# Norms in finer steps in program order, and low parts of weights partly made by adding transfers

## The chip, the cores and the metric

The kernel runs on one NeuronCore of one Trainium2 chip. Its time is device microseconds of one execution. In this text PE is TensorE (PEld its weight loads), DVE is VectorE, ACT is ScalarE, POOL is GpSimd, and SP is SyncE, which issues nearly all loads from HBM.

## What is computed

A two-layer decoder trunk on 544 tokens: 512 of a prompt and 32 of a sample group (8 sequences of 4), model width 1024, feed-forward width 2816. One layer is, with `layer_norm` after each sum:

```python
x = layer_norm(ALPHA * x + 0.5 * swiglu(x, ffn1_up, ffn1_down), ln1)
proj = x @ w_in + b_in                       # queries, keys, values, GLU halves, two gates
attn = window_attention(q, k, v, ...)        # window 128, ALiBi, sinks
c = causal_depthwise(u_a * sigmoid(u_g), conv_dw_w, conv_dw_b)     # 31 taps
c = silu(layer_norm(c, conv_ln))
mix = sigmoid(g_attn) * (attn @ w_attn_out) + sigmoid(g_conv) * (c @ w_conv_out)
x = layer_norm(ALPHA * x + mix @ w_out, ln2)
x = layer_norm(ALPHA * x + 0.5 * swiglu(x, ffn2_up, ffn2_down), ln3)
```

All in float32. The norms run over the model width, which lies on partitions.

## The kernel before

**Arithmetic.** A float32 product is made of three matmuls in a faster 32-bit form (`F32R`): each operand is split into a high part (a cast on ACT) and a low part (operand minus high part, on DVE), and high×high, high×low and low×high are summed in PSUM. Weights come from HBM as float32 in "raw" tiles of 128x1024 (512 KB, 5 buffers), and become a pair of tiles `wh`, `wl`. Activations are kept as pairs too: `X[p]` is the pair for 256 of the 1024 rows of the activations, p from 0 to 3. Nearly all large tiles share one pool, "pair", of 37 buffers.

**Units.** `unit(w, xs, hf)` multiplies one weight piece (256 output columns) with one half `hf` of the tokens: 272 columns in each half. It runs `kk` k-steps (8 for width 1024, 6 for the last group of a feed-forward network) of 6 matmuls each, and it writes one of three double-bank PSUM buffers. At each k-step it first calls `due()`.

**Order.** The Tile scheduler orders the instructions of each engine by a simulation of its own, except where they are pinned to program order. Two devices steer it by hand. `put_off(steps)` puts a list of steps with delays on `self.later`; `due()` calls those whose time has come by `self.clock`, which each k-step advances by 0.7; `flush()` calls whatever is left. And weights are prepared ahead: `W()` loads and splits pieces `la` ahead of use with `prep()`; inside a network `V()`, `fill()`, `step()` do so piece by piece.

**A network and its tail.** A feed-forward network starts with `up_first()`: four pieces (a0, u0, a1, u1; gate and up columns) for both halves of the tokens. Then `middle()` runs fast products (three of seven blocks of a Strassen-like form, pinned) and down units. Its last group, `gl`, has four pieces p of six k-steps, each in two raw tiles of four and two k-rows. They run in `tail()`: units of half 0 with `un(p, 0)`, then units of half 1. Each unit's result is added to `Y[p]` on DVE (L705), and `ln_sum` (L449) sums the `Y[p]`. The tail of `mix()`, behind the output projection, is the same with units of eight k-steps (norm 2).

**A norm** (`ln_fin`) has three steps per half, each with a stop on PE:
- `centre`: fold of the sum (DVE, L461), a matmul with ones for the mean (L463), four subtractions on DVE (L468), four squares on ACT (L472), three adds on DVE (L474);
- `newton`: fold (L481), tiny matmuls with ones (L485), 14 tiny DVE operations of an inverse square root (`rsqrt`, L507 to L521);
- `scale`: matmuls that spread the root (L493), four multiplications on DVE (L497), and per p `emit`: two activations on ACT with gain and bias (L530, for the convolution Silu in L1432), a high part on ACT (L441) and a low part on DVE (L442).

The next network's first units need these pairs: half 0 at once, half 1 four units later. Behind the second network and norm 2, factors `T` for the fast products are made from the normed values (`right`, L549 to L555).

**The norm behind the convolution** (in `mix`). The 30 taps of the depthwise convolution run on DVE (L1081) beside attention and projections. When the last are done, both halves are summed, and their norm runs beside eight units of gate pieces (`gate("gc", p, h)`, sigmoid on ACT in L1358). The output projection of the convolution follows (`co`), and needs all of it as pairs.

Of the kernel before, what the change touches and what calls it, by code (L numbers as in the profile page):

```python
# [24 lines left out]
NT = SEQ + NS  # L25
# [29 lines left out]
A1, A2, A3 = 4, 4, 2  # L55
FOLD = 1
FD = (1.4, 0.7, 2.1)
D_LN = (2.1, 3.5, 2.1)
RS_SEED, RS_A, RS_B = 0x5F1FFFF9, 2.38924456, 0.703952253
SAT = (3, 4, 5, 6, 7, 8, 9, 10)  # L60
TF = 0
# [38 lines left out]
class Ker:  # L100
    def __init__(self, ctx, tc, a):
        self.tc, self.nc, self.a = tc, tc.nc, a
        pool = lambda n, b, **k: ctx.enter_context(tc.tile_pool(name=n, bufs=b, **k))
        self.cp = pool("cp", 1)
        self.fp = pool("fp", FPB)
        self.sp = pool("sp", 4)
        self.wp = pool("wp", WPB)
        self.pp = pool("pp", PPB)
        self.mp = pool("mp", 4)
        self.ps2 = pool("ps2", 3, space=bass.MemoryType.PSUM)  # L110
        self.ps1 = pool("ps1", 2, space=bass.MemoryType.PSUM)
# [46 lines left out]
    def plan(self):  # L158
# [8 lines left out]

        def fast(key, w, j):
# [21 lines left out]
        def ffn(l, f):  # L190
            up, dn = a[f + "_up"][l], a[f + "_down"][l]
            for key in self.ffn_order(l, f):
                if key[0] == "s":
                    fast((l, f) + key, up, key[1])
                elif key[0] == "dn":
                    g, p = key[1:]
                    std((l, f) + key, dn, p * 256, r0=256 * sum(GROUPF[:g]), kk=2 * GROUPF[g])
                else:
                    std((l, f) + key, up, (DFF if key[0] == "u" else 0) + key[1] * 256)
# [93 lines left out]
    def steps(self, key, kk, raw):  # L293
# [19 lines left out]
        if kk:  # L313
            for k, t in enumerate(raw):
                w = t.shape[1] / 4
                out.append((1.0 * w, 0, 2, lambda k=k, t=t: hi(f"d{k}", t)))
                out.append((0, 1.2 * w, 0, lambda k=k, t=t: lo(f"d{k}", t)))
            return out, lambda: self.ready.append((key, [box[f"d{k}"] for k in range(len(raw))], kk))
# [86 lines left out]
    def ahead(self, n):  # L405

        while self.loaded < min(self.pi + n, len(self.pieces)):
            self.prep(True)
# [10 lines left out]
    def unit(self, w, xs, hf, pin=lambda i: i):  # L419
# [31 lines left out]
    def ln_fin(self, acc, Y, hf, emit):  # L451
# [7 lines left out]
        def centre():  # L459
            s = acc[0][:, :, hs]  # L460
            nc.vector.tensor_tensor(s[:, 0], s[:, 0], s[:, 1], op=ALU.add)  # L461
# [7 lines left out]
            for p in range(4):  # L469
# [3 lines left out]
                if p:  # L473
                    nc.vector.tensor_tensor(a, a, q, op=ALU.add)  # L474

        box = {}

        def newton():
            a = acc[1][:, :, hs]
            if FOLD:  # L480
                nc.vector.tensor_tensor(a[:, 0], a[:, 0], a[:, 1], op=ALU.add)  # L481
# [18 lines left out]
        return [(D_LN[0], centre), (D_LN[1], newton), (D_LN[2], scale)]  # L500
# [23 lines left out]
    def ln_out(self, X, l, vg, vb, T=None, func=AF.Identity):  # L524
        vec = self.vec[l]

        def emit(p, y, hs):
            for m in range(2):
                c = 2 * p + m
                self.nc.scalar.activation(y[:, m, hs], y[:, m, hs], func,  # L530
                                          scale=vec[:, vg + c:vg + c + 1], bias=vec[:, vb + c:vb + c + 1])
            xh, xl = X[p]
            self.split(xh[:, :, hs], xl[:, :, hs], y[:, :, hs])
            if T is not None and hs.stop == NT:
                if T:
                    T[-1] = T[-1]()
                T.append(self.right(y))
                if p == 3:
                    T[-1] = T[-1]()
# [37 lines left out]
    def ffn(self, l, f, XYT, vg, vb, last):  # L577
# [11 lines left out]
        def gated(w, h, hf, sa):  # L589
# [3 lines left out]
            self.split(h[0][:, :, hs], h[1][:, :, hs], sa)  # L593
# [6 lines left out]
        def up_first():  # L600
            ws = [self.W(l, f, k, j, la=A1 - 2 * j - (k == "u")) for j in range(2) for k in ("a", "u")]
            hs = [new_h(0) for j in range(2)]
            for hf in range(2):
                for j in range(2):
                    sa = silu(ws[2 * j], hf)
# [6 lines left out]
                    gated(ws[2 * j + 1], hs[j], hf, sa)  # L612
# [121 lines left out]
        up_first()  # L734
# [7 lines left out]
        def pre(hf):  # L742
            if hf == 0:
                ws.extend(self.V(l, f, "dn", gl, p) for p in range(4))
            else:
                self.ahead(A3)
# [4 lines left out]
        return self.tail(un, 0, Y, X, l, vg, vb, pre, f == "ffn2")  # L751
# [25 lines left out]
    def flush(self):  # L777
        for c in self.later:
            for _, fn in c[1]:
                fn()  # L780
        self.later = []

    def put_off(self, steps):
        self.later.append([self.clock + steps[0][0], deque(steps)])

    def tail(self, un, first, Y, XN, l, vg, vb, pre=None, fast=False):

        T = [] if fast else None
        emit = self.ln_out(XN, l, vg, vb, T)
        acc = self.pair(), self.pair()  # L790
        if pre:
            pre(0)
        for p in range(4):
            un(p, 0)
            if p < first:
                un(p, 1)
                self.ln_sum(acc, Y, 1, p)
            self.ln_sum(acc, Y, 0, p)
        self.put_off(self.ln_fin(acc, Y, 0, emit))
        if pre:  # L800
            pre(1)
        for p in range(first, 4):
# [3 lines left out]
        self.put_off(self.ln_fin(acc, Y, 1, emit))  # L806
        return XN, Y, T

    def final(self, un, Y, l, g, b, pre):
# [52 lines left out]
        for hf in range(2):  # L862
            pre(hf)
# [126 lines left out]
    def mix(self, l, XYT):  # L990
# [336 lines left out]
        k_unit(0)  # L1327
        g0[0]()
        g0[2]()
        values(range(2))  # L1330
# [98 lines left out]
        def c_out(p, y, hs):  # L1429
            for m in range(2):  # L1430
                c = 2 * p + m
                nc.scalar.activation(y[:, m, hs], y[:, m, hs], AF.Silu, scale=vec[:, V_CG + c:V_CG + c + 1],  # L1432
                                     bias=vec[:, V_CBETA + c:V_CBETA + c + 1])

        acc = self.pair(), self.pair()
        for hf in range(2):
            for p in range(4):
                self.ln_sum(acc, cl, hf, p)
            self.put_off(self.ln_fin(acc, cl, hf, c_out))
            for p in range(2 * hf, 2 * hf + 2):  # L1440
                for h2 in range(2):
                    gate("gc", p, h2, 36)
        self.flush()
        Y = []
        CH = []
        for p in range(4):
            h, lo = self.hl()
            CH.append((h, lo))
            for hf in range(2):
                self.split(h[:, :, sl(hf)], lo[:, :, sl(hf)], cl[p][:, :, sl(hf)])  # L1450
# [20 lines left out]
        return self.tail(un, TF, Y, XN, l, V_LN2G, V_LN2B, fast=True)  # L1471
# [38 lines left out]
```

## Time and profile before

| | us |
|---|---|
| median of 3 runs | 2594.34 (2584.23 to 2597.09) |
| profiled execution | 2583.82 |
| its span, first to last instruction | 2581.9 |
| PE busy | 2509.8 |
| DVE busy | 1877.7 |
| ACT busy | 1195.0 |
| POOL busy | 238.2 |

The mean granted clock of PE is 0.985 of its full rate; it was lower in short stretches only. PE is busy nearly everywhere, so the places to read are the short stretches in which it isn't. In the order of time those are, for layer 0: the start, the tail of the first network (380 to 420 us), one stretch in attention (near 600), the norm behind the convolution (780 to 820), norm 2 (900 to 940), the tail of the second network (1280 to 1300); layer 1 repeats them 1280 us later, and the kernel ends with `final()`, whose transposes and stores take the place of the last norm.

### The profile page before, as it was taken

The numbers are of one execution on the slowest core, as the hardware profiler recorded it, in microseconds if no ns is written. First come the engines' busy times: TensorE is split into PE (matmuls) and PEld (weight loads), VectorE is DVE, ScalarE is ACT, GpSimd is POOL, SyncE is SP. The second block draws the span as 40 slices with busy tenths as digits, with TensorE's granted clock in tenths as the row PEclk, the third lists the DMA queues.
The fourth block names the chain that finished last, engine by engine and source line by source line (L and its number), as shares of the span: only waits on it lengthen the run. The fifth ranks groups of instructions, "written<-read, shape, count | busy, mean of one in ns | idle before, by whom it ended". The sixth has DMA issues, their size and how long they took to land.

```text
span 2581.9 us, 47139 instructions
## 1 busy us (share of the span) xinstructions
PE 2509.8 (97%) x19846; PEld 2459.2 (95%) x19846; DVE 1877.7 (73%) x2955; ACT 1195.0 (46%) x2116; POOL 238.2 (9%) x323
## 2 busy tenths in 40 slices
PE   8999998999999999999899999999999999999997
PEld 8999998988999999999899999999899999999997
DVE  6766665997976577666667666669979666776665
ACT  4444434577426254434354434346873353444441
POOL 2000000722300000000100000016141000000000
PEclk9999999999999999999999999999999999999998
DMA  5333332231332223332503332322224222233321
GB/s 193 98 99 99 99 109 59 69 95 54 90 95 67 82 75 98 99 99 86 183 17 107 94 94 87 114 66 75 70 62 111 66 82 88 78 97 99 99 86 56
DMA packets 327140, 232.13 MB, mean 90 GB/s; under 512 B 43748, under 2 KB 324532, under 8 KB 326832
## 3 DMA queue, kind: packets, MB, share of 16 engines
q1 hardware_dynamic: 323088, 220.36, 28.6%
q0 software_dynamic: 3840, 8.76, 1.0%
q8 instruction: 155, 2.54, 0.4%
q14 instruction: 57, 0.47, 0.1%
HBM read 225.69 MB, written 9.16 MB: 91 GB/s over the span
## 4 chain that ended last, share of the span: by engine, by line
PE 84%; DVE 8%; ACT 3%; POOL 3%; issue 1%; DMA 1%; DVEq 0%; POOLq 0%; ACTq 0%
PE pa L652 17%; PE pa L432 17%; PE pa L434 17%; PE pa L433 17%; PE pb L652 13%; DVE pr L1081 3%; POOL f L1096 2%; DVE wl L278 1%; PE pa L1192 1%; PE pb L1221 1%; PE pb L1233 1%; DVE pr L442 1%; DVE pr L497 1%; ACT pr L1432 0%; ACT at L1206 0%
## 5 line engine op out<-in xcount | busy, mean ns | idle before, releaser
L432 PE MATMUL pa<-pr,wh 128*128 128x272 f32 x2624 | 766.0, 294 | 22.5 <-ACT pr L441 18.7
L434 PE MATMUL pa<-pr,wl 128*128 128x272 f32 x2624 | 764.2, 292 | 4.4 <-DVE wl L278 4.4
L433 PE MATMUL pa<-pr,wh 128*128 128x272 f32 x2624 | 761.3, 291 | 5.8 <-DVE pr L442 5.8
L432 PEld LDWEIGHTS pa<-pr,wh 128*128 128x128 f32 x2624 | 497.8, 190 | 30.1 <-ACT pr L441 21.8
L433 PEld LDWEIGHTS pa<-pr,wh 128*128 128x128 f32 x2624 | 501.4, 191 | 10.6 <-DVE pr L442 8.2
L434 PEld LDWEIGHTS pa<-pr,wl 128*128 128x128 f32 x2624 | 497.8, 190 | 5.3 <-DVE wl L278 5.0
L434 PE MATMUL pa<-pr,wd 128*128 128x272 f32 (+2 forms) x1408 | 406.9, 289 | 0.0
L432 PE MATMUL pa<-pr,wd 128*128 128x272 f32 (+2 forms) x1408 | 404.9, 288 | 0.0
L433 PE MATMUL pa<-pr,wd 128*128 128x272 f32 (+2 forms) x1408 | 404.6, 288 | 0.0
L1081 DVE SCALAR_TENSOR_TENSOR pr<-u,cw,pr 128x512 f32<-128x512 f32 x480 | 345.4, 769 | 2.0 <-ACT pr L1074 1.7
L433 PEld LDWEIGHTS pa<-pr,wd 128*128 128x128 f32 x1408 | 266.1, 189 | 0.0
L434 PEld LDWEIGHTS pa<-pr,wd 128*128 128x128 f32 x1408 | 264.5, 188 | 0.1
L432 PEld LDWEIGHTS pa<-pr,wd 128*128 128x128 f32 x1408 | 264.4, 188 | 0.2
L652 PE MATMUL pa<-pr,wa 128*128 128x272 f32 x1728 | 241.4, 289 | 0.0
L652 PE MATMUL pb<-pr,ws 128*128 128x272 f32 x1728 | 239.4, 288 | 0.0
L278 DVE TENSOR_TENSOR wl<-raw,wh 128x1024 fp32r<-128x1024 f32 x168 | 205.0, 1239 | 33.2 <-ACT wh L277 32.5
L652 PEld LDWEIGHTS pa<-pr,wa 128*128 128x128 f32 x1728 | 227.1, 188 | 0.0
L652 PEld LDWEIGHTS pb<-pr,ws 128*128 128x128 f32 x1728 | 224.9, 188 | 0.0
L277 ACT CAST wh<-raw 128x1024 fp32r<-128x1024 f32 x168 | 171.2, 1048 | 88.5 <-PE pa L433 36.1
L705 DVE SCALAR_TENSOR_TENSOR pr<-pa,pr 128x544 f32<-128x544 f32 (+2 forms) x160 | 115.3, 723 | 132.0 <-PE pa L434 130.4
L670 ACT COPY pb<-pa 128x272 f32<-128x272 f32 x72 | 26.6, 370 | 294.9 <-PE pa L652 294.9
L442 DVE TENSOR_TENSOR pr<-f,pr 128x544 fp32r<-128x544 f32 x124 | 89.1, 723 | 82.1 <-ACT pr L441 82.0
(226 smaller groups left out, 3741.8 us busy)
## 6 DMA issues: line engine op xcount, KB each, us to landing
raw<-in_ffn_up_dram SPq DMA_DIRECT2D x174, 512.0 KB, 4.0
raw<-in_ffn_down_dram SPq DMA_DIRECT2D x80, 512.0 KB, 3.4
raw<-in_w_in_dram SPq DMA_DIRECT2D x72, 512.0 KB, 3.9
raw<-in_w_in_dram SPq DMA_DIRECT2D x64, 128.0 KB, 2.9
raw<-in_w_attn_out_dram SPq DMA_DIRECT2D x32, 256.0 KB, 4.0
raw<-in_w_conv_out_dram SPq DMA_DIRECT2D x16, 512.0 KB, 3.5
raw<-in_w_out_dram SPq DMA_DIRECT2D x16, 512.0 KB, 4.4
raw<-in_ffn_down_dram SPq DMA_DIRECT2D x16, 256.0 KB, 2.7
```

The lines of the kernel that those rows point to most:

```text
L277: ins = self.nc.scalar.copy(wh, t)
L278: self.nc.vector.tensor_tensor(wl, t, wh.bitcast(F32), op=ALU.subtract)
L432: pin(self.nc.tensor.matmul(o, lhsT=wh, rhs=h, start=k == 0, stop=False))
L433: pin(self.nc.tensor.matmul(o, lhsT=wh, rhs=lo, start=False, stop=False))
L434: pin(self.nc.tensor.matmul(o, lhsT=wl, rhs=h, start=False, stop=k == kk - 1))
L442: pin(self.nc.vector.tensor_tensor(lo, src, hi.bitcast(F32), op=ALU.subtract))
L497: nc.vector.tensor_tensor(y[:, :, hs], y[:, :, hs], rb, op=ALU.mult)
L652: mm = lambda a, b, first=False, last=False: pin(nc.tensor.matmul(o, lhsT=a, rhs=b, start=first, stop=last, skip_group_check=True))
L670: pin(act.copy(A, b1))
L705: pin(nc.vector.scalar_tensor_tensor(Y[p][:, :, hs], ps, 0.5, Y[p][:, :, hs], op0=ALU.mult, op1=ALU.add))
L1081: self.last["cw"] = nc.vector.scalar_tensor_tensor(cc[:, m, 0:SEQ], u[:, m, k:k + SEQ], cw[:, 8 * k + c:8 * k + c + 1], cc[:, m, 0:SEQ], o ...
L1096: nc.gpsimd.tensor_tensor(pr[:, 4 * b:4 * b + 4, :], win, wv.unsqueeze(1).to_broadcast([128, DS, KC]), op=ALU.mult)
```

## The change

- **Program order.** A context `ordered()` makes each PE, DVE and ACT instruction inside it depend on the one traced before it on its engine, so the scheduler can't move it. It covers every tail, `up_first()` of every network but the first, the first units behind norm 1 in `mix` (keys, first GLU piece, first values), and the eight gate units with the convolution's norm.
- **Finer steps.** Tails start each half's norm after that half's units, with delays `D_T` instead of `D_LN`; both halves of the convolution's norm start together with delays `D_C` (the second's first delay is 14.0). The low parts of the normed values are no longer made in `emit`, but as four steps of their own (`D_LO`), and the factors `T` as five more (`D_R`). Folds move one step earlier: into `ln_sum` at p = 3, and to the end of `centre`. The convolution's pairs `CH` are made in its `emit` and not behind the flush. `flush()` now takes the remaining steps in order of time. A k-step advances the clock by 0.75.
- **Next weights.** `early()` loads the next piece and gives a step for each of its two tiles. In the tails of networks, one piece is split ahead of the units, with its low parts on DVE. Three more (six tiles, in every tail) are made at clock values `when` in the second half's units, at their end, and in the next network's first units, each in this way: ACT casts the high part, ACT writes minus the tile in the fast form to `wl`, and a transfer issued by POOL adds the raw tile to it in place.
- **Twin pieces.** Of the last down group, the two-row tiles of pieces p and p+1 are loaded into one raw tile by two transfers, so that two pieces have three tiles and not four.

```diff
+    @contextmanager
+    def ordered(self):
+        traced = self.nc.cur_bb.bb.instructions
+        start = len(traced)
+        last = {}
+        for i in traced:
+            last[i.engine] = i
+        self.hard = True
+        yield
+        self.hard = False
+        for i in traced[start:]:
+            if i.engine in (mybir.EngineType.PE, mybir.EngineType.DVE, mybir.EngineType.Activation):
+                self.tc.add_manual_dep(
+                    i, last[i.engine].name,
+                    mybir.DependencyInfo(mybir.DependencyClass.NoSync, mybir.DependencyReason.DATA), reason="ordered")
+            last[i.engine] = i
...
+D_T = ((2.6, 5.6, 4.0), (3.4, 5.6, 4.0))
+D_C = ((0.8, 5.6, 4.0), (14.0, 5.6, 4.0))
+D_LO = (1.7, 1.4, 1.4, 1.4)
+D_R = 2.0
...
+    def early(self, by_dma=True):
+        key, kk, raw = self.fetch()
+        ms = []
+        def one(t, end):
+            wh, wl = (self.pp.tile(list(t.shape), F32R, tag="pair", name=self.nm(n)) for n in ("wh", "wl"))
+            self.nc.scalar.copy(wh, t)
+            if by_dma:
+                self.nc.scalar.mul(wl, t, -1.0)
+                self.nc.gpsimd.dma_start(wl.bitcast(F32), t, accum_op=ALU.add)
+            else:
+                self.nc.vector.tensor_tensor(wl, t, wh.bitcast(F32), op=ALU.subtract)
+            ms.append((wh, wl))
...
-            self.clock += 0.7
+            self.clock += 0.75
...
+        if p == 3:
+            self.nc.vector.tensor_tensor(a[:, 0], a[:, 0], a[:, 1], op=ALU.add)
...
-            xh, xl = X[p]
-            self.split(xh[:, :, hs], xl[:, :, hs], y[:, :, hs])
...
+            h, lo = (x[:, :, hs] for x in X[p])
+            self.nc.scalar.copy(h, y[:, :, hs])
+            lows.append(lambda: self.nc.vector.tensor_tensor(lo, y[:, :, hs], h.bitcast(F32), op=ALU.subtract))
...
+    def tail_steps(self, un, Y, XN, l, vg, vb, when, first, T):
+        acc = self.pair(), self.pair()
+        def fin(hf):
+            lows = []
+            steps = self.ln_fin(acc, Y, hf, self.ln_out(XN, l, vg, vb, lows), D_T[hf])
+            steps += [(d, lambda i=i: lows[i]()) for i, d in enumerate(D_LO)]
+            if hf and T is not None:
...
+                steps += [(D_R, lambda i=i: factors(i)) for i in range(5)]
+            self.put_off(steps)
+        if first:
+            for fn in self.early(False):
                 fn()
         for p in range(4):
             un(p, 0)
             self.ln_sum(acc, Y, 0, p)
+        fin(0)
+        more = []
+        def tile():
+            if not more:
+                more.extend(self.early())
+            more.pop(0)()
+        for w in when:
+            self.put_off([(w, tile)])
+        for p in range(4):
             un(p, 1)
             self.ln_sum(acc, Y, 1, p)
         self.flush()
+        fin(1)
+        if more:
+            self.put_off([(1.0, tile)])
+        self.put_off([(4.5, tile), (0.1, tile)])
         return XN, Y, T
...
-        return self.tail(un, 0, Y, X, l, vg, vb, pre, f == "ffn2")
+        return self.tail(un, Y, X, l, vg, vb, (7.0, 9.5, 18.2), True, f == "ffn2")
...
+        with self.ordered():
+            for hf in range(2):
+                lows = []
+                steps = self.ln_fin(acc, cl, hf, c_out(lows), D_C[hf])
+                self.put_off(steps + [(d, lambda i=i, lows=lows: lows[i]()) for i, d in enumerate(D_LO)])
+            for p in range(4):
                 for h2 in range(2):
                     gate("gc", p, h2, 36)
-        self.flush()
+            self.flush()
...
-        return self.tail(un, TF, Y, XN, l, V_LN2G, V_LN2B, fast=True)
+        return self.tail(un, Y, XN, l, V_LN2G, V_LN2B, (7.0, 18.3, 24.2), False, fast=True)
```

## Rows read from the trace of the kernel before

**Rows 1.** The page, part 1: busy us (share of the span) xinstructions

```profile
PE 2509.8 (97%) x19846; PEld 2459.2 (95%) x19846; DVE 1877.7 (73%) x2955; ACT 1195.0 (46%) x2116; POOL 238.2 (9%) x323
```

**Rows 2.** Waits of PE: line, releaser, us in total, times, longest us

```profile
PE pa L432 <- ACT pr L441: 18.7, 7, 2.9
PE pb L493 <- DVE nw L521: 11.0, 3, 3.8
PE pb L485 <- DVE pr L481: 3.7, 3, 1.9
```

**Rows 3.** Windows of 20 us: busy us (instructions), granted clock, DMA share, GB/s

```profile
core 0: us, PE busy (x) PEld busy (x) DVE busy (x) ACT busy (x) POOL busy (x), PEclk, DMA share, GB/s
380.00:400.00 20.00, 14.27 (x112) 13.50 (x110) 15.65 (x36) 5.33 (x9) 0.15 (x1) 0.93 0.33 92
400.00:420.00 20.00, 17.71 (x122) 17.39 (x123) 13.24 (x29) 13.94 (x24) 0.00 (x0) 0.81 0.09 20
420.00:440.00 20.00, 19.86 (x162) 19.69 (x161) 10.48 (x16) 9.52 (x18) 0.00 (x0) 1.00 0.51 139
480.00:500.00 20.00, 19.91 (x174) 18.07 (x173) 19.90 (x45) 14.88 (x39) 18.96 (x25) 1.00 0.14 31
780.00:800.00 20.00, 19.11 (x155) 18.91 (x154) 13.10 (x29) 19.31 (x29) 0.00 (x0) 1.00 0.16 53
800.00:820.00 20.00, 17.15 (x127) 16.93 (x127) 14.29 (x18) 11.01 (x18) 0.00 (x0) 0.91 0.33 106
900.00:920.00 20.00, 19.43 (x149) 18.63 (x148) 16.65 (x22) 12.12 (x18) 0.00 (x0) 1.00 0.51 155
920.00:940.00 20.00, 16.94 (x136) 16.51 (x135) 12.63 (x31) 10.57 (x17) 0.00 (x0) 1.00 0.01 5
1280.00:1300.00 20.00, 10.77 (x54) 9.40 (x53) 16.32 (x37) 8.51 (x16) 0.00 (x0) 0.66 0.24 74
```

**Rows 4.** Timeline of DVE near 393: start, us, line, operation, out<-in, count

```profile
393.01 0.72 DVE L449 TENSOR_TENSOR pr<-pr,pr 128x544 f32<-128x544 f32 x1
...
397.28 2.62 DVE L497 TENSOR_TENSOR pr<-pr,pb 128x544 f32<-128x544 f32 x4 [1.06 <-PE pb L493]
```

**Rows 5.** Timeline of PE at 396, the spreading of the root

```profile
396.37 0.87 PE L493 MATMUL pb<-ident,nw 91*128 91x91 f32 x6 [3.75 <-DVE nw L521]
```

**Rows 6.** Timeline of DVE at 890: first and last of 14 Newton operations

```profile
890.06 0.16 DVE L507 TENSOR_SCALAR nw<-pb 91x3 f32<-91x3 f32 x1 [0.68 <-PE pb L485]
...
892.40 0.16 DVE L521 TENSOR_TENSOR nw<-nw,nw 91x3 f32<-91x3 f32 x1
```

**Rows 7.** Timeline of ACT, 760 to 810: squares, sigmoid, table load, Silu, copy

```profile
761.01 1.22 ACT L472 ACTIVATE f<-pr 128x544 f32<-128x544 f32 x2
...
771.00 0.87 ACT L1358 ACTIVATE pr<-pa,vec 128x272 f32<-128x272 f32 x2 [3.76 <-PE pa L434]
771.89 1.28 ACT L1432 ACT_TABLE_LOAD   x1
...
807.27 2.13 ACT L1432 ACTIVATE pr<-pr,vec 128x272 f32<-128x272 f32 x4
809.30 0.63 ACT L441 CAST pr<-pr 128x544 fp32r<-128x544 f32 x1
```

**Rows 8.** The page, part 5: low and high part of a weight tile

```profile
L278 DVE TENSOR_TENSOR wl<-raw,wh 128x1024 fp32r<-128x1024 f32 x168 | 205.0, 1239 | 33.2 <-ACT wh L277 32.5
L277 ACT CAST wh<-raw 128x1024 fp32r<-128x1024 f32 x168 | 171.2, 1048 | 88.5 <-PE pa L433 36.1
```

**Rows 9.** DMA issues of POOL's queue: count, KB each, median us to landing

```profile
out_new_conv_sample_dram<-in_state_conv_dram POOLq DMA_DIRECT2D x2, 832.0 KB, 12.5
at<-in_ln_g_dram POOLq DMA_DIRECT2D x1, 512.0 KB, 3.9
```

**Rows 10.** Timeline of POOL at 486: eight issues

```profile
485.74 4.20 POOL L1133 DMA_DIRECT2D out_new_v_sample_dram<-f  x8
```

**Rows 11.** Timeline of DVE ahead of the convolution's norm, 739 to 753

```profile
739.93 0.72 DVE L1424 TENSOR_TENSOR pr<-pa,f 128x544 f32<-128x544 f32 x1 [0.70 <-PE pa L434]
...
748.67 1.53 DVE L1081 SCALAR_TENSOR_TENSOR pr<-u,cw,pr 128x512 f32<-128x512 f32 x2
...
751.51 0.79 DVE L461 TENSOR_TENSOR pr<-pr 128x272 f32<-128x272 f32 x2
```

More of the change, by code (lines that the diff above doesn't have):

```diff
@@ L1 @@
 from collections import deque
[L2 removed]
+from contextlib import ExitStack, contextmanager
 import numpy as np
@@ L317, in steps, with whole @@
                 out.append((0, 1.2 * w, 0, lambda k=k, t=t: lo(f"d{k}", t)))
-            return out, lambda: self.ready.append((key, [box[f"d{k}"] for k in range(len(raw))], kk))
+            def whole():
+                ms = [box[f"d{k}"] for k in range(len(raw))]
+                if key[2] == "dn" and key[3] == len(GROUPF) - 1:
+                    if kk == 4:
+                        ms.append([x[:, 2:] for x in self.twin])
+                    else:
+                        self.twin = ms[1]
+                self.ready.append((key, ms, 6 if key[2] == "dn" and key[3] == len(GROUPF) - 1 else kk))
+            return out, whole
         La, Lu = raw
@@ L403, in after @@
                 mybir.DependencyInfo(mybir.DependencyClass.NoSync, mybir.DependencyReason.DATA), reason=key)
-    def ahead(self, n):
-        while self.loaded < min(self.pi + n, len(self.pieces)):
-            self.prep(True)
+    def early(self, by_dma=True):
[7 more added lines that the diff above has]
+                self.nc.gpsimd.dma_start(wl.bitcast(F32), t, accum_op=ALU.add)
+            else:
+                self.nc.vector.tensor_tensor(wl, t, wh.bitcast(F32), op=ALU.subtract)
+            ms.append((wh, wl))
+            if end:
+                self.ready.append((key, ms, kk))
+        return [lambda t=t, end=i == len(raw) - 1: one(t, end) for i, t in enumerate(raw)]
     def W(self, *key, la=LA):
@@ L592, in gated @@
             nc.vector.tensor_tensor(sa, ps, sa, op=ALU.mult)
-            self.split(h[0][:, :, hs], h[1][:, :, hs], sa)
+            if self.hard and not hf:
+                hh, hl = (x[:, :, hs] for x in h)
+                nc.scalar.copy(hh, sa)
+                self.put_off([(0.8, lambda: nc.vector.tensor_tensor(hl, sa, hh.bitcast(F32), op=ALU.subtract))])
+            else:
+                self.split(h[0][:, :, hs], h[1][:, :, hs], sa)
         def new_h(g):
@@ L733, in ffn @@
         turn = self.mark(l, f)
-        up_first()
+        if Y0:
+            with self.ordered():
+                up_first()
+                self.flush()
+        else:
+            up_first()
         Y += self.scaled(Y0)
@@ L740, in ffn, with pre @@
         ws = []
[L742 to L746, printed above, removed]
+        def pre():
+            ws.extend(self.V(l, f, "dn", gl, p) for p in range(4))
         un = lambda p, hf: down_unit(ws[p], gl, p, hf)
@@ L1326, in mix @@
         g0, g1, g2, g3 = (glu(p) for p in range(4))
[L1327 to L1330, printed above, removed]
+        with self.ordered():
+            k_unit(0)
+            g0[0]()
+            g0[2]()
+            values(range(2))
+            self.flush()
         k_unit(1)
@@ L1427, in mix, with c_out, emit @@
         cl = [C[p] for p in range(4)]
[L1429 to L1433, printed above, removed]
+        CH = [self.hl() for _ in range(4)]
+        def c_out(lows):
+            def emit(p, y, hs):
+                for m in range(2):
+                    c = 2 * p + m
+                    nc.scalar.activation(y[:, m, hs], y[:, m, hs], AF.Silu, scale=vec[:, V_CG + c:V_CG + c + 1],
+                                         bias=vec[:, V_CBETA + c:V_CBETA + c + 1])
+                h, lo = (x[:, :, hs] for x in CH[p])
+                nc.scalar.copy(h, y[:, :, hs])
+                lows.append(lambda: nc.vector.tensor_tensor(lo, y[:, :, hs], h.bitcast(F32), op=ALU.subtract))
+            return emit
         acc = self.pair(), self.pair()
```

102 lines of the change are left out of this document (55 added, 47 removed).

## The prediction

> **What bounds the kernel now.** The page's first part comes first: TensorE (PE) is busy 97% of the span, 2509.8 of 2581.9 us [rows 1]. So a change can win only where PE stands still or runs at its lower clock level. The waits of PE name such places [rows 2]: the first matmul of a unit waits for an activation's high part made by ScalarE (ACT), 18.7 us; a norm's last matmul waits for the Newton steps on VectorE (DVE), 11.0 us; the sum of squares comes late, 3.7 us. All belong to norms. Sizes come from the windows of 20 us [rows 3]. A full window holds 162 matmuls, so one costs 0.1235 us; a unit of eight k-steps (48 matmuls) costs 5.93, one of six 4.45, a step 0.74. Missing matmuls times 0.1235 is the loss, the clock included (granted 0.66 in the window at 1280, between the levels 1.2 and 2.4 GHz):
> - behind a first feed-forward network, 380 to 420: 90 missing, 11.1 us (twice, once a layer);
> - behind the second network of layer 0, 1280 to 1300: 108 missing, 13.3 us;
> - norm 2, 900 to 940: 39 missing, 4.8 us (twice);
> - norm of the convolution, 780 to 820: 42 missing, 5.2 us (twice).
> That is 55.5 us, the most there is to win.
>
> **Prices.** On half the columns a DVE add takes 0.72 (0.65 back to back, as in 2.62 for four) [rows 4]. The norm's own three stops cost PE about half a microsecond each (0.87 for six of the last stop, of two halves) [rows 5]. The 14 Newton operations take 2.5 us from first to last [rows 6]. On ACT a square costs 0.6, a 272-column activation 0.53, the copy of a high part about 0.54 where the next pass overlaps it: 1.6 for a pair [rows 7]. A weight tile costs 1.05 on ACT (high part) and, up to now, 1.24 on DVE (low part) [rows 8].
>
> **The tails behind the networks.** Before, the scheduler placed the first half's Newton and scale behind all units, so both halves' norms stood bare: DVE's L497 comes at 397, after PE's 3.75 us wait [rows 4, 5]. In the change PE must take them between k-steps at stated clock values. I put zero at the end of the first half's units, six k-steps each. Output add, sum, fold: 0.15 (hand-over, an estimate)+0.72+0.72+0.44, ready at 2.1; PE asks at 2.96. Four subtractions, squares behind each, three adds, fold: ready at 8.7; PE asks at 9.4. Newton runs 11.0 to 13.5 behind the second unit's two adds; PE asks at 14.4. Nothing waits. Multiplications 16.0 to 18.6, ACT's four pairs 16.7 to 23.1. The next network's first unit starts at 19.25 and needs pair 2's low part at 22.35; its subtraction stands in program order behind the last unit's output add and sums and ends at 22.95: **0.6 us of wait**. Second half: the early weight tile moved to the end of the units and its neighbour hold ACT from 23.1 to 27.2 (2.05 each: a cast and a multiplication by -1); the squares queue behind them, the sum is ready at 30.9 and PE asks at 30.05: **0.9 us**. Later steps have slack. I put 1.6 for a tail: two gain 11.1-1.6, together 19.0; the one at 1280 gains 11.7. Norm 2 has units of eight steps, 5.9 us more before the next network, and the same sums leave no wait; I allow 0.3, so 4.8-0.3 twice, 9.0. Moving DVE folds one step earlier costs nothing by itself: the 0.44 is in the sums above; without cover it would be 0.44 at a stop.
>
> **Low parts by transfers.** Six tiles in each of five tails leave DVE (1.24 each) and cost ACT about 1.05 more, a GpSimd (POOL) issue, and an adding transfer SBUF to SBUF, 512 KB. The trace has no such transfer. Below: 3.9 us, the plain load of the same size on that queue; above: 12.5, the longest that queue takes to land [rows 9]. It reads its destination too, so I take 6, near the row with the same queue and bytes. The third piece's tiles leave ACT at 25.1 and 27.2 and are needed at 33.6 and 36.6; the fourth's at 31.7 and 33.8, needed at 40.0 and 41.5. The least slack is 7.7: **no cost at 6**; at 12.5 about 4 us a tail. Below nothing: taking 1.24 off DVE could gain only where DVE ends a wait, which the sums already have. On POOL nothing but the convolution's clear and small state products is queued near them; SP's weight loads keep their order, but a raw buffer is held until its transfer lands, and the last of those loads has over 5 us in hand. The POOL queue issued eight transfers in 4.20 us, 0.52 each, while DVE was busy 19.90 of 20 us [rows 3, 10].
>
> The Trainium skill, "SBUF — State Buffer", section "SBUF: two separate sides" (its trap "DVE blocks DMA"), speaks against this: a DMA issued by GpSimd can starve for descriptors while DVE holds the shared port, 620 ns becoming 3,100. By it each issue is 2.5 us later, by estimate 8.5 to land and up to 0.8 us of wait a tail, 4 us in all. The row shows no such delay.
>
> **Twin pieces** (the last group's two short tiles loaded as one): 6 tiles instead of 8 a network, the same bytes and elements, four pair buffers fewer. I cost it at nothing: the window at 380 has 4.35 us of DVE and 14.7 of ACT idle to cover it [rows 3]; without that cover it is one cast, 1.05. The new clock step of 0.75 matches the 0.74 measured. The first two units' low parts put off by 0.8 are needed two units later: nothing.
>
> **The norm behind the convolution.** Here strict order cuts the other way. The last convolution taps keep DVE until 750.2 and the sums until 752.3 [rows 11], while the first gate unit starts near 745.8 (739.9 plus a unit). In the change the low parts of the second gate piece (2.4) move behind those sums, in program order ahead of the norm: sums end near 749.9, 4.1 after the unit's start; low parts 6.5; subtractions 9.1; adds and fold 11.7. PE asks for the mean after two k-steps and for the sum of squares at 7.9, and **waits 3.9 us** over the two. Second half, from the start of the third gate unit: sigmoid 0.9, two casts until 3.0, their low parts on DVE until 4.4, only then the first half's multiplications; the table load (1.28) hides, ACT's eight Silu and four copies run 5.1 to 11.5 [rows 7]. The second half's squares stand behind them: 11.5 to 13.9, fold 15.1. PE asks at 9.1 and **waits 6.0 us**. Behind PE are two gate units' sigmoids and nothing else that is late. Waits of such length cost clock: 0.91 of the window at 800 is 1.8 us lost [rows 3]; I add 2. So 12 replaces 5.2: a loss of 6.8, twice, 13.6. Its bounds: 0 (the taps end earlier and the sums with them, and ACT is free) and 17 (clock as at 1280, 6.8 lost). I take 12, since the taps run 4.4 us past the start of the gates [rows 11].
>
> **Sum.** 19.0+11.7+9.0-13.6 = 26.1. The profiled execution took 2583.8 (span 2581.9 and 1.9 around it), so 2557.7, say **2558**. The profiled time equals the lowest of the three runs, 10.5 below their median; a median of the changed kernel may lie as much above my number.
>
> **Rivals.**
> (A) The convolution's norm becomes free too. For: it now has eight gate units, 47 us, for two chains of 16. Against: the order of Silu and squares. No wait left: 2583.8-39.7-10.4 = 2534.
> (B) In-order waits eat half of the tails' gain: an ACT cast waiting for a raw tile holds the squares behind it. For: ACT carries 2.05 per early tile; against: five raw buffers and the slack above. 2583.8-19.9+13.6 = 2577.
> (C) Slower: the adding transfers run one behind another. Four tiles follow from 25.1, the last is needed at 41.5; the gain of 26 over five tails, 5.2 each, is gone when they land 5.4 us apart. At 6.5 apart a tail waits 9.6 us: 2583.8-26.1+48 = 2606. Against: the 3.9 us row includes latency that overlaps.
> (D) The order changes nothing that PE feels, because the scheduler's order already had it: 2584. Against: L497 at 397.
>
> **Chances.** Forecast 0.46 (2548 to 2568), A 0.28, B 0.12, D 0.06, C 0.08. Half a per cent, 13 us, is what a measurement here can tell from no change. Faster: 0.44+0.28+0.03 = 0.75; same 0.17; slower 0.08. Range 2530 to 2588: A with a few microseconds below, and B and D above; C is left out.
>
> **What would show it.** Windows as above: 380 to 420 and 1280 to 1300 with at most some 13 matmuls missing, clock 1.00; L497 of the first half well before the units end. In the convolution's norm PE should wait for DVE's L481 by about 4 and 6 us, Silu ahead of the squares on ACT. If that wait is absent, A; if PE waits for a DMA or low parts of weights, C; if for ACT casts, B. The prediction is wrong if PE waits at places without a norm, because buffers or loads moved.

## The result and the profile after

The changed kernel takes 2565.7 us beside 2594.8 before (medians of four executions each): a ratio of 0.989, 95% interval 0.985 to 0.993. One of its executions ran at a granted clock of 0.68 and took 3336.9 us; it counts in that median and not in the ratio, and the other three lie between 2561.5 and 2567.3, their median at 2564.1. The profiled execution took 2564.1 us (span 2562.3), 19.7 below that of before; the forecast was 26.1 below, at 2558.

The profile of the changed kernel: from its first part (busy us, share of the span, instructions), its DMA queues (packets, MB, share of 16 engines) and its DMA issues (count, KB each, median us to landing).

```profile
PE 2501.2 (98%) x19846; PEld 2454.7 (96%) x19846; DVE 1853.9 (72%) x2917; ACT 1229.7 (48%) x2138; POOL 266.5 (10%) x353
...
q0 software_dynamic: 8160, 24.49, 4.3%
...
L459 POOL DMA_DIRECT2D wl<-raw x30 | 26.4, 881 | 1303.4 <-DVE pr L534 947.4
...
wl<-raw POOLq DMA_DIRECT2D x30, 512.0 KB, 5.7
```

PE's busy time fell 8.6 us against [rows 1] and the span 19.6, so 11 us of what was won is time in which PE stood still and the rest is time in which it ran slowly. The adding transfers, which no row of before showed, are 30 and land in 5.7 us.

PE's waits in the changed kernel (line and releaser, us in total, times, longest). In its numbering L508 is the fold ahead of the mean, L534 the fold ahead of the sum of squares, L579 the last Newton operation, L592 the low part of a normed value, and L313 the low part of a weight tile:

```profile
PE pb L543 <- DVE pr L534: 17.2, 7, 6.5
PE pa L491 <- DVE wl L313: 6.4, 3, 3.9
PE pa L995 <- DMA at<-in_x_prompt_dram: 4.6, 1, 4.6
PE pb L521 <- DVE pr L508: 4.4, 2, 2.2
...
PE pb L551 <- DVE nw L579: 2.6, 2, 1.3
```

Of the waits in [rows 2], that for ACT's high parts (18.7) has left the head of the list, and that for Newton (11.0) is down to 2.6. The wait for the sum of squares has grown from 3.7 to 17.2, and that for the mean is new. Windows of 20 us say where (PE busy and matmuls first, granted clock third from the end):

```profile
380.00:400.00 20.00, 19.31 (x155) 19.01 (x155) 16.46 (x37) 13.80 (x21) 1.87 (x2) 1.00 0.52 118
400.00:420.00 20.00, 18.03 (x146) 17.66 (x145) 11.51 (x30) 17.03 (x27) 3.61 (x5) 1.00 0.95 188
740.00:760.00 20.00, 16.65 (x130) 16.05 (x129) 14.67 (x33) 6.72 (x11) 0.00 (x0) 1.00 0.17 54
760.00:780.00 20.00, 13.49 (x97) 13.30 (x95) 13.08 (x31) 12.93 (x23) 0.00 (x0) 0.83 0.17 53
900.00:920.00 20.00, 20.00 (x162) 19.92 (x161) 12.89 (x31) 14.98 (x19) 4.33 (x5) 1.00 0.93 205
...
1280.00:1300.00 20.00, 18.69 (x148) 18.20 (x147) 14.56 (x34) 16.21 (x24) 5.22 (x7) 1.00 0.87 209
```

Against [rows 3], the tail at 380 to 420 misses 23 matmuls instead of 90, that at 1280 14 instead of 108, and norm 2 none. The convolution norm now misses 97, 12.0 us, with the clock at 0.83, where it missed 42.

Both traces hold 19846 matmuls in the same order of stages, so the start of the nth one in each, subtracted, gives the gain by stage. This is the table that the rest of the section leans on (us, changed minus before; the kernel in which strict order is off is an experiment below):

| stage | forecast | changed | order off |
|---|---|---|---|
| first network's tail, layers 0 and 1 | -9.5, -9.5 | -8.8, -9.2 | -0.3, +0.6 |
| second network's tail, layer 0 | -11.7 | -12.4 | -1.9 |
| norm 2, layers 0 and 1 | -4.5, -4.5 | -5.0, -5.0 | +3.7, +3.4 |
| convolution norm, layers 0 and 1 | +6.8, +6.8 | +6.9, +8.3 | +9.7, +9.6 |
| attention, layers 0 and 1 | 0, 0 | +1.9, +3.0 | 0, -1.6 |
| start | 0 | +0.7 | +2.6 |

The tails come to 40.4 won against 39.7 forecast, the convolution norm to 15.2 lost against 13.6. Attention, costed at nothing, lost 4.9. The stages of the experiments below are taken in the same way.

### The profile page after: what moved, and what is told of

It reads as the page before. It is cut to its first block, busy times and chain, and to the rows that moved or that the text cites. A ratio compares the mean times of both kernels' runs of the same rounds, so it can differ in the third digit from the quotient of the medians.

```text
span 2562.3 us, 47210 instructions
## 1 busy us (share of the span) xinstructions
PE 2501.2 (98%) x19846; PEld 2454.7 (96%) x19846; DVE 1853.9 (72%) x2917; ACT 1229.7 (48%) x2138; POOL 266.5 (10%) x353
## 4 chain that ended last, share of the span: by engine, by line
PE 83%; DVE 8%; ACT 5%; POOL 2%; issue 1%; DMA 0%; DVEq 0%; POOLq 0%; ACTq 0%
PE pa L718 17%; PE pa L489 16%; PE pa L491 16%; PE pa L490 16%; PE pb L718 13%; DVE pr L1181 3%; POOL f L1196 2%; DVE wl L313 1%; PE pa L1292 1%; PE pb L1321 1%; DVE at L1302 1%; PE pb L1333 1%; ACT pr L588 0%; DVE pr L499 0%; ACT at L1306 0%
## 5 line engine op out<-in xcount | busy, mean ns | idle before, releaser
L313 DVE TENSOR_TENSOR wl<-raw,wh 128x1024 fp32r<-128x1024 f32 x132 | 160.9, 1239 | 41.7 <-ACT wh L312 41.3
L312 ACT CAST wh<-raw 128x1024 fp32r<-128x1024 f32 x132 | 133.9, 1050 | 59.0 <-PE pa L491 27.1
L459 POOL DMA_DIRECT2D wl<-raw x30 | 26.4, 881 | 1303.4 <-DVE pr L534 947.4
```

What stands on the lines that cost most here:

```text
L312: ins = self.nc.scalar.copy(wh, t)
L313: self.nc.vector.tensor_tensor(wl, t, wh.bitcast(F32), op=ALU.subtract)
L459: self.nc.gpsimd.dma_start(wl.bitcast(F32), t, accum_op=ALU.add)
```

## The experiments

Line numbers are those of the changed kernel; with order off they are 6 lower, with the transfers made twice 1 higher, with the attention's low parts by transfer 4 higher.

**The convolution norm put back.** One part of the change undone:

```diff
         for hf in range(2):
             for p in range(4):
                 self.ln_sum(acc, cl, hf, p)
-        with self.ordered():
-            for hf in range(2):
-                lows = []
-                steps = self.ln_fin(acc, cl, hf, c_out(lows), D_C[hf])
...
+            self.put_off(self.ln_fin(acc, cl, hf, c_out))
+            for p in range(2 * hf, 2 * hf + 2):
                 for h2 in range(2):
                     gate("gc", p, h2, 36)
...
+        self.flush()
```

> The norm behind the convolution is put back to what it was before the change (scheduler's own order, old delays, low parts of its output by one subtraction a pair and half after the norm); tails, norm 2, twin pieces and adding transfers stay changed. Theory (strict order costs the convolution norm; nth-matmul starts of the two traces put its loss at 6.9 and 8.3 us in the two layers): the changed kernel's 2565.7 less 15 gives about 2551 us (2547 to 2555), TensorE's waits for line 534 of 6.5 us are gone, and 740 to 780 us misses no more than the 40 or so matmuls that before missed. Rival (TensorE only arrives 8 us sooner there, at convolution taps on VectorE that are no sooner done, so any form of this norm waits): 2561 to 2566 us, and a wait of TensorE of 4 us or more for VectorE is left in 735 to 780.

It took 2543.5 us, ratio 0.9806 (0.9791 to 0.9820), 22 below the changed kernel. The norm now costs 1.3 us a layer less than before, so 17.8 of the 20.9 us between the two profiled spans come from there and 2.9 from attention. Waits of PE from 735 to 830:

```profile
PE pa L489 <- ACT pr L498: 2.8, 1, 2.8
PE pb L543 <- DVE pr L534: 0.9, 1, 0.9
```

The rival falls: PE arrived some 7 us sooner than before and found the taps no obstacle. The theory holds in its cause; the time is 3.5 us below its range, since attention and the 1.3 us a layer came on top.

**The stops moved, order kept.**

```diff
-D_C = ((0.8, 5.6, 4.0), (14.0, 5.6, 4.0))
+D_C = ((4.5, 7.5, 9.0), (9.0, 8.25, 9.75))
```

> Strict order is kept; only the stops of the convolution norm move: first half's mean at 4.5 (0.8) on the planner's clock, second half's mean 9.0 (14.0), each Newton 7.5 and 8.25 later (5.6), scaling 9.0 and 9.75 later (4.0), so that the squares of both halves are asked of ScalarE before the first half's Silu. Theory (the order of squares behind Silu, and a mean asked before its sums are there, make the waits): the 2.2 us for line 508 and the 1.2 and 6.5 us for line 534 fall to under 1.5 us in all, the granted clock stays at 1.0 in 760 to 780, some 10 to 11 us a layer come back: 2544 us (2541 to 2552). Rival (low parts of the next gate piece and late taps hold VectorE there, wherever the stops are): the waits move but 5 us or more a layer stay, 2558 us or more.

2543.5 us, ratio 0.9807 (0.9791 to 0.9823). The norm costs 0.6 and 0.7 us more than before, not 6.9 and 8.3, so 6.3 and 7.6 us came back and not 10 to 11; the total fits because attention, too, took 6.6 us less in this execution. One wait is left from 735 to 830, and the granted clock falls behind it. The profile names a gate's sigmoid (L1460), which stands on ACT behind the second half's Silu and casts:

```profile
PE pa L489 <- ACT pr L1460: 4.4, 1, 4.4
...
760.00:780.00 20.00, 20.00 (x163) 20.00 (x162) 11.17 (x25) 14.03 (x22) 0.00 (x0) 1.00 0.18 56
780.00:800.00 20.00, 15.64 (x113) 15.42 (x112) 12.87 (x13) 17.04 (x26) 0.00 (x0) 0.91 0.23 72
```

So strict order by itself costs this norm 0.7 us a layer at most; the numbers in D_C cost the rest.

**One stop moved.** To split the loss, only the second half's mean:

```diff
-D_C = ((0.8, 5.6, 4.0), (14.0, 5.6, 4.0))
+D_C = ((0.8, 5.6, 4.0), (9.0, 5.6, 4.0))
```

> The changed kernel with one number of the convolution norm moved: the second half's mean at 9.0 on the planner's clock (14.0), so that its squares are asked of ScalarE just before the first half's Silu (its scaling is asked at 10.4) and not behind it. Theory (of the loss there the longest wait, 6.5 us, is the squares behind 6.3 us of Silu and casts): that wait falls to under 1.5, the waits of the first half (2.2 for line 508, 1.2 for line 534) stay, and the clock in 760 to 780 goes from 0.83 to 0.95 or more: 7 to 9 us a layer, 2565.7 less 16 gives 2550 us (2546 to 2554). Rival (the first half's mean, asked at 0.8 before its sums are there, is what puts all later stops late): the 6.5 us wait becomes 4 us or more elsewhere, 2558 us or more.

2549.4 us, ratio 0.9825 (0.9811 to 0.9840), the theory's time, though in part by luck, as the stages below show. Here is ACT in the changed kernel, from the first half's Silu (L1537) to the second half's squares (L530), and PE behind it:

```profile
761.44 1.12 ACT L1537 ACTIVATE pr<-pr,vec 128x272 f32<-128x272 f32 x2 [0.81 <-DVE pr L555]
...
767.69 0.65 ACT L1540 CAST pr<-pr 128x544 fp32r<-128x544 f32 x1
768.24 0.65 ACT L530 ACTIVATE pr<-pr 128x544 f32<-128x544 f32 x1
768.80 1.73 ACT L530 ACTIVATE f<-pr 128x544 f32<-128x544 f32 x3
...
772.48 1.05 PE L543 MATMUL pb<-ones,pr 128*91 128x1 f32 x6 [6.51 <-DVE pr L534]
```

and ACT with the one stop moved:

```profile
753.30 0.66 ACT L530 ACTIVATE pr<-pr 128x544 f32<-128x544 f32 x1 [5.22 <-DVE pr L526]
753.94 1.98 ACT L530 ACTIVATE f<-pr 128x544 f32<-128x544 f32 x3
...
760.87 1.12 ACT L1537 ACTIVATE pr<-pr,vec 128x272 f32<-128x272 f32 x2 [1.01 <-DVE pr L555]
```

The squares stand ahead of Silu, and the wait of 6.5 us is gone. What PE still waits for from 735 to 830 are the two waits of the first half that the theory left standing, and one of 2.1 us for the second half's Newton that it had not foreseen:

```profile
PE pb L521 <- DVE pr L508: 2.2, 1, 2.2
PE pb L551 <- DVE nw L579: 2.1, 1, 2.1
PE pb L543 <- DVE pr L534: 1.2, 1, 1.2
```

By stage the norm lost 2.2 and 2.3 us here, so this one number of D_C cost 4.7 and 6.0 us, where the theory had 7 to 9 a layer. The rest of the difference, some 5 us, is attention, which lost nothing in this execution; the theory had no part in that.

**Order off.** The dependencies left out, the steps and delays kept:

```diff
         self.hard = False
-        for i in traced[start:]:
-            if i.engine in (mybir.EngineType.PE, mybir.EngineType.DVE, mybir.EngineType.Activation):
-                self.tc.add_manual_dep(
...
-            last[i.engine] = i
```

> The changed kernel without the dependencies that hold TensorE, VectorE and ScalarE to program order; the finer steps, the delays, twin pieces and adding transfers stay. Theory (program order is what places a step where its stop is): the ends of the networks and norm 2 lose most of their 40 us again, the convolution norm wins its 15, about 2590 us (2578 to 2605), with waits of TensorE for ScalarE or VectorE of 2 us and more back at 380 to 420 and 1280 to 1300. Rival (the finer steps and longer delays do it, order adds nothing but the loss at the convolution): 2551 us (2546 to 2558), no wait over 1.5 us in the tails.

2609.8 us, ratio 1.0063 (1.0048 to 1.0078): slower than before, and slower than the theory's range. The tails lose all that they had won and 5.5 us more (last column of the table). Waits of PE from 370 to 430:

```profile
PE pb L545 <- DVE nw L573: 4.0, 1, 4.0
PE pa L483 <- ACT pr L585: 2.5, 1, 2.5
PE pa L484 <- DVE pr L586: 1.3, 1, 1.3
```

These are the waits of [rows 2] again, for Newton and for a high part. But half of the theory failed: the convolution norm did not win its 15. It lost 9.7 us a layer without order, more than with it, and at another place: from 735 to 830 PE waits 10.1 us for L1454, a gate's sigmoid behind Silu on ACT, and 1.4 for L1534, a cast of the norm's output.

**Old delays, order on.**

```diff
-D_T = ((2.6, 5.6, 4.0), (3.4, 5.6, 4.0))
+D_T = (D_LN, D_LN)
```

> The changed kernel with the old delays 2.1, 3.5, 2.1 at the five norms of the tails, strict order and all else kept. Theory (order makes each stop binding, so the longer delays are needed): Newton's matmul is asked 2.1 us sooner than now and waits 2 us or more, the spread 1.9 us sooner and waits 2 us or more, in each of the halves: 4 us for each half of five norms, 40 us lost, 2600 us (2585 to 2610). Rival (order alone, whatever the delays, gives the gain): 2566 us, within 5.

2593.0 us, ratio 1.0001 (0.9992 to 1.0010). The five tails win 10.1 us instead of 40.4. From 380 to 430 the waits are now at the stops themselves:

```profile
PE pb L543 <- DVE pr L534: 3.4, 2, 1.7
PE pb L551 <- DVE nw L579: 2.2, 2, 1.8
```

The theory's 4 us for each half was too much (30.3 over ten halves is 3.0), its direction right. Order with the old delays gives a quarter of the gain, the new delays without order none.

**Low parts on DVE again.**

```diff
-                more.extend(self.early())
+                more.extend(self.early(False))
```

> The changed kernel with the six low parts a tail that are made by adding transfers (a negated copy on ScalarE and a transfer) made by VectorE instead, at the same stops. Theory (VectorE is busy for some 27 of 40 us in a tail and the low parts are put between the norm's steps; what the transfers take off it is idle time or up to 1.2 us ahead of one step): within 1 us a tail, 2566 us (2561 to 2571). Rival (VectorE's queue is what the transfers free; each low part delays a step that TensorE waits for): 2 to 3 us a tail more, 2576 to 2580.

2569.5 us, ratio 0.9913 (0.9898 to 0.9928). The total fits the theory, but by accident: the three network tails win 5.8, 6.3 and 6.0 us instead of 8.8, 12.4 and 9.2, together 12.3 less, and the stages between them happened to lose less in this execution. DVE in the first tail:

```profile
397.41 0.44 DVE L508 TENSOR_TENSOR pr<-pr 128x272 f32<-128x272 f32 x1
399.60 1.23 DVE L461 TENSOR_TENSOR wl<-raw,wh 128x1024 fp32r<-128x1024 f32 x1 [1.75 <-ACT wh L456]
400.75 1.35 DVE L592 TENSOR_TENSOR pr<-pr,pr 128x544 fp32r<-128x544 f32 x2
402.02 1.22 DVE L461 TENSOR_TENSOR wl<-raw,wh 128x1024 fp32r<-128x1024 f32 x1
403.15 2.61 DVE L526 TENSOR_TENSOR pr<-pr,pb 128x544 f32<-128x544 f32 x4
```

A weight tile's low part (L461) waits for its cast, which stands behind the first half's output on ACT. In program order the norm's own low parts (L592) and the second half's subtractions (L526) stand behind it, and PE waits 3.7 us for L592. So the rival's mechanism is real: what the transfers take away is an instruction that stands in the way on DVE, which is worth more than its 1.24 us of work.

**Each transfer made twice.**

```diff
-            self.nc.scalar.mul(wl, t, -1.0)
+            self.nc.scalar.mul(wl, t, -2.0)
             self.nc.gpsimd.dma_start(wl.bitcast(F32), t, accum_op=ALU.add)
+            self.nc.gpsimd.dma_start(wl.bitcast(F32), t, accum_op=ALU.add)
```

> The changed kernel with each adding transfer made twice, one behind the other on the same tile (the copy is negated and doubled, so the low parts come out doubled: this part of the computation is changed), so that a low part lands some 11.4 us after its issue and not 5.7. Theory (slack least 7.7 us by the trace of before): 0 to 4 us a tail, some 10 in all, 2576 us (2568 to 2586), with TensorE waiting for a transfer. Rival (the slack is larger, transfers are free even at double length): 2566 us, within 3, no wait for a transfer.

2607.5 us, ratio 1.0059 (1.0040 to 1.0078), 42 above the changed kernel, four times the theory's price. PE's waits in the whole span, and POOL in the first tail:

```profile
PE pa L492 <- DMA wl<-raw: 22.6, 13, 4.5
...
PE pb L1224 <- DMA wl<-raw: 10.1, 4, 4.8
...
411.47 2.13 POOL L459 DMA_DIRECT2D wl<-raw  x2
412.54 1.21 POOL L1124 MEMSET u<- 128x60 f32 x1
419.03 0.87 POOL L460 DMA_DIRECT2D wl<-raw  x1 [5.28 <-DMA wl<-raw]
423.79 0.87 POOL L460 DMA_DIRECT2D wl<-raw  x1 [3.89 <-DMA wl<-raw]
```

The second transfer of a tile waits on POOL for the first to land, and that of the next tile waits behind it: the last issue comes at 423.8, where the changed kernel's last issue stood at 408.1. This execution ran some 3 us later by then, so the last issue moved by some 12 us and not by 5.7. The run doesn't say at which lateness the slack ends. It does show what the slower rival of the prediction costs where it is made to happen: it had put 2606 on it.

**Three tries at a faster kernel.** From the moved stops, each with more stops read off the trace before it:

```diff
 closer convolution stops:
+D_C = ((4.5, 7.5, 6.0), (9.0, 7.5, 6.75))
 stops by the trace:
+D_C = ((4.5, 7.5, 7.5), (9.0, 7.5, 6.75))
+D_T = ((2.6, 5.6, 5.5), (3.4, 5.6, 4.0))
 closer stops and a late spread:
+D_C = ((4.5, 7.5, 6.0), (9.0, 7.5, 6.75))
+D_T = ((2.6, 5.6, 4.0), (3.4, 5.6, 5.5))
```

> As the kernel with the moved convolution stops (2543.5 us, wait of 4.4 us a layer left, where TensorE's first product of the convolution's output waits for the second half's Silu and casts), with the scaling of the first half 6.0 after its Newton step (9.0) and that of the second 7.5 and 6.75 (8.25 and 9.75), so that the second half is scaled before the third gate piece's low parts are asked. Theory (what is left is second-half scaling on VectorE behind low parts whose casts stand behind the first half's Silu on ScalarE): the 4.4 us wait goes to under 1, the clock in 780 to 800 to 1.0 from 0.91: 2534 us (2531 to 2538). Rival (ScalarE's 14 us of Silu in one go stop the gate's sigmoids, and TensorE waits for a free PSUM tile instead): 2543 us or more, a wait of TensorE's gate products for line 1460.

> Strict order with stops read off the traces: convolution norm as in the kernel with closer stops, but the first half's scaling 7.5 after Newton (6.0), and the scaling of the first half in the five tail norms 5.5 after Newton (4.0). Theory (each wait of TensorE for line 565 or 579, 1.7 us a layer in the convolution norm and 1.3 us in the two first-network tails, is a stop set too soon and goes when it is set later): some 6 us less than 2538.6: 2533 us (2529 to 2538). Rival (a later scaling only moves the wait on to the second half or to what needs the output): 2538 us or more.

> The kernel with closer convolution stops (2538.6 us), with the scaling of the second half of the five tail norms 5.5 after Newton (4.0); the kernel with stops by the trace had moved that of the first half, which has no wait. Theory (TensorE's wait of 1.3 us for line 579 in the two first-network tails is the second half's spread): it goes, 2.6 us less, within what the timing can tell: 2536 us (2533 to 2541). Rival (it moves to the first product that needs the scaled output): 2538 to 2544 us, a wait of 1 us or more for line 592 or 588.

The first took 2538.6 us, ratio 0.9791 (0.9776 to 0.9806), the lowest of all; the wait of 4.4 us is gone, one of 1.7 for Newton came (L551), which keeps it above the theory's range (2531 to 2538), and the norm costs about 1.5 us a layer less than before. The second took 2544.4 (0.9821, 0.9808 to 0.9835): the 1.7 us fell to 0.2 and 2.3 us came, for a cast of gate weights behind the Silu; the wait of 1.3 us in the tails stayed (1.4), since it is for the second half, whose stop had not moved. The third took 2552.5 (0.9833, 0.9817 to 0.9850): the wait of 1.3 us in the first tail went, and from 380 to 430 stands

```profile
PE pb L1133 <- DVE at L1227: 3.1, 1, 3.1
```

for work of the attention's head on DVE; that it now stands behind the norm's later steps in program order is the likely reason, not a tested one. Both theories fell. The second kernel's rival held, and the third took longer than its own rival had put: in both, a wait of 1 to 2 us came back at another place when a stop was set later.

**Attention's low parts by transfer**, on top of the stops by the trace:

```diff
-            m, ins = self.halves(t, list(t.shape))
+            m, ins = self.halves(t, list(t.shape), by_dma=key[1] == "ao" or key[1:] in (("ga", 2), ("ga", 3)))
```

> The kernel with stops by the trace, and also the low parts of the attention output's four weight pieces and of the last two attention gate pieces made by adding transfers and no longer by VectorE. Theory (at the attention's end VectorE is busy without a gap, and TensorE waits 1.8 us, or 3.9 us when VectorE was held for 5.79 us beside GpSimd, for such a low part): that wait goes in both layers, VectorE comes to the convolution taps 6 to 9 us sooner: 4 to 6 us less than the kernel beside it. Rival (the transfers are issued by GpSimd, whose products beside a busy VectorE take 9.65 us; TensorE waits for the transfer instead, as with the transfers made twice): 3 us or more slower than the kernel beside it.

2543.7 us, ratio 0.9817 (0.9804 to 0.9831), beside 2544.4: no difference. The wait of 1.8 us in each layer became 0.6 for the transfer and 0.5 for ACT; by stage attention wins 2.2 us in layer 0 and loses 1.8 in layer 1 against the kernel beside it. Neither theory nor rival.

## Why the prediction came out as it did

**The tails: right in mechanism and size.** 39.7 forecast, 40.4 measured. The two waits named for a first-network tail are there, 0.69 for L592 (0.6 forecast) and 0.64 for L534 (0.9). A third was not foreseen: 1.33 us for the second half's Newton, which stands on DVE behind an activation's low part (L499) that waited 3.45 us for ACT's cast:

```profile
409.23 0.72 DVE L499 TENSOR_TENSOR pr<-f,pr 128x544 fp32r<-128x544 f32 x1 [3.45 <-ACT pr L498]
```

Hence 23 matmuls missing at 380 to 420 and not 13. Norm 2, allowed 0.3 of wait, has none. The two experiments on delays and order show that the steps' work as a whole carries this: neither alone does.

**The convolution norm: right in size and in its longest wait, too wide in its cause.** The waits were put at 3.9 and 6.0 us; measured 3.4 (2.2 and 1.2) and 6.5, with the 12 us of loss exact in layer 0. The place was right too: squares behind Silu on ACT. But the step began with "Here strict order cuts the other way", and that failed: with order kept and other stops the norm loses 0.7 us a layer or wins 1.5, and without order the same stops lose 9.7. The loss belongs to the stops in D_C. Of these the second half's mean at 14.0 was moved alone and accounts for 4.7 and 6.0 us; the mean at 0.8 and the later delays were only moved together. Whether the wait of the first half came from low parts of the gate piece ahead of the norm, as the step said, was not tried by itself: in the kernel with moved stops they stand there still, and nobody waits.

**Adding transfers: size right, price of the alternative left out.** Taken at 6 us to land, measured 5.7 (4.4 to 8.8). The Trainium skill, "SBUF — State Buffer", section "SBUF: two separate sides", would have had 8.5, by the estimate in the prediction. Its trap speaks of DVE operations in a two-port mode, a condition that the prediction didn't name; no trace shows the mode of an operation. The trace has no delay of 2.5 us at an issue: the 30 took 0.85 to 0.98 us each. Why the slowest landed in 8.8 stays open. An issue took 0.88 us on average, not the 0.52 of [rows 10], whose eight transfers move 4 KB each. No wait of PE for a transfer stands in the profile after, so they cost nothing, as forecast. The step also said that taking the low parts off DVE could gain only where DVE ends a wait; with the low parts left on DVE in strict order DVE ends one in each network tail, and taking them off is worth 12 us of the 40. The sum had it silently, by leaving them out of DVE's chain. At a landing of 12.5 us it put 4 us a tail; transfers made twice cost some 10 a tail, because of the queue on POOL.

**Attention at nothing: wrong by 4.9 us**, the largest miss of the sum (26.1 less 19.6). The prediction's own mark for this was PE waiting at places without a norm. In layer 0 the wait for a weight's low part from 620 to 720 is 3.9 us instead of 1.8, 2.1 us more; the last section shows what went with it in that execution, and it did not happen in most others. Another 1.5 us went behind that wait: the granted clock fell to 0.65 from 666 to 670, where it stayed at 1.00 before. An earlier stretch won 1.6 back. In layer 1 the same wait is 1.8 as before, but the clock behind it fell to 0.64 (1929 to 1933; 1.00 before), again 1.5 us, and the other 1.6 lie in the window from 1840 to 1860, of which the same work before stands at 1860 to 1880:

```profile
1840.00:1860.00 20.00, 20.00 (x125) 17.41 (x125) 8.54 (x19) 13.12 (x38) 0.00 (x0) 0.74 0.21 66
...
1860.00:1880.00 20.00, 19.47 (x139) 16.23 (x140) 12.61 (x26) 16.19 (x45) 0.00 (x0) 0.88 0.21 66
```

With the moved stops the clock of this work was 0.91, and behind the wait of 1.8 us 1.00. PE's instructions there are the same in both kernels, so the level seems to change from run to run; what sets it stays open. So of the 4.9 us some 2 are a longer wait and the rest is clock; no wait for a buffer or a load, which the mark had named, stands there.

**Rivals.** The first, a convolution norm that is free too, at 2534, needed only other stops: 2538.6 measured. The second, in-order waits that eat half of the tails' gain, did not come; the low parts on DVE show a wait of that kind, on DVE and not on ACT, and at smaller size (12.3 us). The fourth, that the order changes nothing, falls: the first half's multiplications (L555) come at 390.3 instead of 397.3, five us ahead of the last unit's output add. Twin pieces, the low parts as steps of their own and the new clock step were not tried alone.

## What to carry to other kernels

In this kernel a chain of small steps between matmuls needed both a stop late enough for its inputs and an order that keeps the stop in its place; test each alone before crediting either. With engines in program order, look at what is queued behind the waiting instruction, and ask of an activation chain (Silu, table loads) which short step of another chain stands behind it: one stop moved by 5 us of planned time brought 4.7 and 6.0 us. Split a measured gain by stage before crediting it: two experiments here met their forecast in part because attention ran 5 to 7 us faster. When the last waits were of 1 to 2 us, setting stops later shifted them, in both tries; then take the best measured version.

## What the runs showed of the hardware that was not expected

In these traces DVE and POOL slow each other when both work on elementwise operations, and which of the two loses more differs from run to run. In layer 0 of the changed kernel one convolution tap on DVE, otherwise some 0.75 us, took 5.79, while POOL ran 13 products, 0.49 each:

```profile
644.50 5.79 DVE L1181 SCALAR_TENSOR_TENSOR pr<-u,cw,pr 128x512 f32<-128x512 f32 x1
...
643.35 6.36 POOL L1196 TENSOR_TENSOR f<-f,cw 128x124 f32<-128x124 f32 x13
```

The same 13 products in the kernel with moved stops, where DVE and POOL have the same instructions in the same order up to there:

```profile
644.57 9.64 POOL L1196 TENSOR_TENSOR f<-f,cw 128x124 f32<-128x124 f32 x13
```

There POOL's products take 0.74 each, and the DVE taps among them 0.91 to 1.02, none of them long. Of the 13 traces of this case three show the held tap (changed, closer stops, old delays), each with 5.79 and 6.36, and those three alone have PE's wait of 3.9 us at 620 to 720; the others with DVE making these low parts have 1.8. That is a correlation over 13 runs and was not forced by an experiment. The longer wait is worth some 2 us, and 3.6 with the lower clock that followed it in all three, about the difference between versions that a tuner would want to tell apart here.
